# Softmax on one core: whole-tile blocks with one broadcast multiply, one row in eight on ScalarE, and two loads dealt out unevenly

## The chip, the cores and the metric

The kernel runs on one core of a Trainium2 chip. The metric is the time of one execution on the device in microseconds (us), the median of several runs. The work is done by two compute engines, VectorE (DVE in the profile) and ScalarE (ACT), and by 16 DMA engines that move data between the main memory (HBM) and the on-chip memory (SBUF, 128 partitions). Transfers are issued by SyncE (SP, all loads) and by ScalarE (all stores). TensorE and GpSimd do nothing here.

## The reference

`x` has 16 x 1024 rows of 512 float32 values. Each row is divided by a temperature of 0.5 and put through softmax.

```python
def setup_inputs():
    batch, seq, dim = 16, 1024, 512
    return {
        "x": np.random.randn(batch, seq, dim).astype(np.float32),
    }

def reference(x: np.ndarray) -> np.ndarray:
    temp = 0.5
    x_scaled = x / temp
    x_max = np.max(x_scaled, axis=-1, keepdims=True)
    exp_x = np.exp(x_scaled - x_max)
    return (exp_x / np.sum(exp_x, axis=-1, keepdims=True)).astype(np.float32)
```

33.55 MB are read and 33.55 MB written.

## The kernel before

The 16,384 rows are cut into eight tiles (`c` = 0 to 7) of 4 MB. In a tile each of the 128 partitions holds `G` = 16 consecutive rows of 512 values, 32 KB that are contiguous in HBM too. All work is done in place in the tile `xt`; the pool `data` has six such buffers, so tiles 0 to 5 can be loaded at once, and the load of tile 6 has to wait until tile 0 has been stored, that of tile 7 until tile 1 has been.

A tile is worked on in blocks: tile 0 in blocks of 4, 4 and 8 rows, the others in two blocks of 8 rows. For a block there are five steps.

- `shift` (VectorE): one reduce gives the negated maximum of every row (L65), and a small multiply by 2 turns it into a bias (L67).
- `exponentials` (ScalarE): one ACTIVATE a row computes exp(2x + bias) in place and adds the row up into `sums` (L75).
- `scale_vector` (VectorE): a reciprocal of the sums (L89), then one TENSOR_SCALAR a row that multiplies by it (L91), for three rows in four.
- `scale_scalar` (ScalarE): the rest, one row in four, by an ACTIVATE with Copy and a scale (L98).
- `store` (issued on ScalarE's queue, L105): when the tile's last block is done, one 4 MB transfer.

The order is written out by hand: each engine works through its instructions in the order in which the program gives them. The loop runs over the blocks, and each later step lags behind:

```python
for i in range(n + 3):
    if i < n:
        if blocks[i][1] == 0:
            load(blocks[i][0])
        shift(i)
        exponentials(i)
    if 1 <= i <= n:
        scale_vector(i - 1)
    if 2 <= i <= n + 1:
        scale_scalar(i - 2)
    if 3 <= i:
        store(i - 3)
```

So on VectorE the order is shift of block i, scale of block i-1; on ScalarE it is exponentials of block i, Copies of block i-2, store of block i-3. The loads stand alone on SP's queue (L59): tile 0 in three transfers of 1, 3 and 12 rows a partition, the other tiles in one. Transfers signal their end over eight semaphores that loads and stores take in turn; the framework adds the waits.

Of the kernel before, what the change touches and what calls it, by code (L numbers as in the profile page):

```python
# [1 line left out]

# [4 lines left out]


@with_exitstack
def kernel(  # L10
    ctx: ExitStack,
    tc: tile.TileContext,
    x: bass.AP,
    out: bass.AP,
):
    nc = tc.nc
    fp32 = mybir.dt.float32
    P = nc.NUM_PARTITIONS
    AX = mybir.AxisListType.X
    EXP = mybir.ActivationFunctionType.Exp  # L20
    COPY = mybir.ActivationFunctionType.Copy
    MAX = mybir.AluOpType.max

    D = x.shape[-1]
    xf = x.flatten_outer_dims()
    of = out.flatten_outer_dims()
    N = xf.shape[0]

    G = 16
    C = N // (P * G)
    assert C * P * G == N
    xr = xf.rearrange("(c p g) d -> c p g d", p=P, g=G)
    outr = of.rearrange("(c p g) d -> c p g d", p=P, g=G)

    FIRST = [(0, 1), (1, 4), (4, 16)]
    BLOCKS_FIRST = [(0, 4), (4, 4), (8, 8)]
    BLOCKS = [(0, 8), (8, 8)]  # L40

    data = ctx.enter_context(tc.tile_pool(name="data", bufs=6))
    stats = ctx.enter_context(tc.tile_pool(name="stats", bufs=6))

    ctx.enter_context(tc.manual_schedule())


    warm = stats.tile([P, 1], fp32, name="warm", bufs=1)
    nc.vector.memset(warm, 0.0)  # L49
    nc.scalar.activation(out=warm, in_=warm, func=EXP)  # L50

    tiles = {}
    blocks = [(c, b, B) for c in range(C) for b, B in (BLOCKS if c else BLOCKS_FIRST)]
    state = {}

    def load(c):
        xt = tiles[c] = data.tile([P, G, D], fp32, name="xt")
        for lo, hi in FIRST if c == 0 else [(0, G)]:
            nc.sync.dma_start(out=xt[:, lo:hi, :], in_=xr[c][:, lo:hi, :])  # L59

    def shift(i):
        c, b, B = blocks[i]
        xb = tiles[c][:, b : b + B, :]
        negmax = stats.tile([P, 8], fp32, name="negmax")
        nc.vector.tensor_reduce(negmax[:, 0:B], xb, axis=AX, op=MAX, negate=True)  # L65
        bias = stats.tile([P, 8], fp32, name="bias")
        nc.vector.tensor_scalar_mul(bias[:, 0:B], negmax[:, 0:B], 2.0)  # L67
        state[i] = (xb, bias)

    def exponentials(i):  # L70
        B = blocks[i][2]
        xb, bias = state[i]
        sums = stats.tile([P, 8], fp32, name="sums")
        for g in range(B):
            nc.scalar.activation(  # L75
                out=xb[:, g, :],
                in_=xb[:, g, :],
                func=EXP,
                bias=bias[:, g : g + 1],
                scale=2.0,  # L80
                accum_out=sums[:, g : g + 1],
            )
        state[i] = (xb, sums)

    def scale_vector(i):
        B = blocks[i][2]
        xb, sums = state[i]
        recip = stats.tile([P, 8], fp32, name="recip")
        nc.vector.reciprocal(recip[:, 0:B], sums[:, 0:B])  # L89
        for g in range(B - B // 4):  # L90
            nc.vector.tensor_scalar_mul(xb[:, g, :], xb[:, g, :], recip[:, g : g + 1])  # L91
        state[i] = (xb, recip)

    def scale_scalar(i):
        B = blocks[i][2]
        xb, recip = state[i]
        for g in range(B - B // 4, B):
            nc.scalar.activation(  # L98
                out=xb[:, g, :], in_=xb[:, g, :], func=COPY, scale=recip[:, g : g + 1]
            )  # L100

    def store(i):
        c, b, B = blocks[i]
        if b + B == G:
            nc.scalar.dma_start(out=outr[c], in_=tiles[c])  # L105

    n = len(blocks)
    for i in range(n + 3):
        if i < n:
            if blocks[i][1] == 0:  # L110
                load(blocks[i][0])
            shift(i)
            exponentials(i)
        if 1 <= i <= n:
            scale_vector(i - 1)
        if 2 <= i <= n + 1:
            scale_scalar(i - 2)
        if 3 <= i:
            store(i - 3)


# [1 line left out]
_INS = ['x']  # L123
_OUTS = [((16, 1024, 512), 'float32')]


# [23 lines left out]
```

## Time and profile before

| | |
|---|---|
| median of 9 runs | 162.86 us (162.54 to 163.09) |
| the profiled execution's own time | 163.02 us |
| span of the profiled execution | 161.2 us |
| VectorE busy | 114.0 us (71%), 148 instructions |
| ScalarE busy | 113.1 us (70%), 290 instructions |
| data moved by the DMA engines | 67.13 MB, mean 417 GB/s |
| time in packets, share of 16 engines' span | loads 49.4%, stores 48.2% |
| transfers | 10 loads issued on SP, 8 stores issued on ScalarE |

The span is the stretch that the profile covers, from the first to the last instruction; the time has some 1.8 us more around it. A busy share is an average over the whole span. A queue's share is the time that its packets took, over the time of all 16 DMA engines: 100% for loads and stores together would be engines that are never without a packet. In the lines below, "x16" is a number of instructions, "128x512" partitions by elements, and "<-" names what ended a wait.

### The profile page before, as it was taken

What the parts mean: (1) busy time and instruction counts of PE and PEld (TensorE: products, weight loads), DVE (VectorE), ACT (ScalarE), POOL (GpSimd) and SP (SyncE); (2) the same over time, 40 slices, a digit from 0 to 9 for tenths busy, and PEclk for the clock granted to TensorE, in tenths of its full rate; (3) what the DMA queues carried; (4) which work ended last, traced back from release to release, by engine and by line L of the source; (5) the groups of instructions that cost most, each with busy time, mean ns of one, the idle gap of its engine ahead of it and who ended that gap; (6) DMA issues with size and microseconds to landing.
All of it is one profiled execution on the core that took longest, in us unless ns stands there. A gap on an engine that the chain in (4) does not pass through costs nothing.

```text
span 161.2 us, 519 instructions
## 1 busy us (share of the span) xinstructions
DVE 114.0 (71%) x148; ACT 113.1 (70%) x290; POOL 0.2 (0%) x4
## 2 busy tenths in 40 slices
DVE  0507999999999999999999938997099956000000
ACT  3071579989999999999999994699808999200000
POOL 0000000000000000000000000000000000000000
DMA  5999999999999999999999999999999999999993
GB/s 175 476 407 488 407 399 496 409 398 488 407 301 464 392 447 455 399 439 455 407 425 472 407 415 480 407 415 480 407 415 472 415 415 455 431 415 455 431 415 130
DMA packets 2595, 67.13 MB, mean 417 GB/s; under 512 B 288, under 2 KB 288, under 8 KB 544
## 3 DMA queue, kind: packets, MB, share of 16 engines
q1 hardware_dynamic: 1440, 33.56, 49.4%
q10 hardware_dynamic: 1152, 33.55, 48.2%
q14 instruction: 3, 0.02, 0.0%
HBM read 33.55 MB, written 33.55 MB: 416 GB/s over the span
## 4 chain that ended last, share of the span: by engine, by line
DMA 43%; DVE 34%; ACT 7%; issue 1%; SPq 1%
DMA xt<-in_x_dram 25%; DVE negmax L65 23%; DMA out_dram<-xt 19%; DVE xt L91 9%; ACT xt L75 5%; ACT xt L98 2%; DVE bias L67 1%; SPq L59 1%; DVE recip L89 0%
## 5 line engine op out<-in xcount | busy, mean ns | idle before, releaser
L75 ACT ACTIVATE xt<-xt,bias 128x512 f32<-128x512 f32 x128 | 90.5, 708 | 24.2 <-DVE bias L67 24.2
L65 DVE TENSOR_REDUCE negmax<-xt 128x8 f32<-128x4096 f32 (+1 forms) x17 | 70.8, 4165 | 17.9 <-DMA xt<-in_x_dram 17.9
L91 DVE TENSOR_SCALAR xt<-xt,recip 128x512 f32<-128x512 f32 x96 | 39.6, 482 | 0.6
L75 ACT ACTIVATION_READ_ACCUMULATOR xt<-xt,bias 128x1 f32 x128 | 23.9, 187 | 0.0
L98 ACT ACTIVATE xt<-xt,recip 128x512 f32<-128x512 f32 x32 | 21.0, 707 | 0.0
L89 DVE RECIPROCAL recip<-sums 128x8 f32<-128x8 f32 (+1 forms) x17 | 3.3, 193 | 3.2 <-ACT xt L75 3.2
L67 DVE TENSOR_SCALAR bias<-negmax 128x8 f32<-128x8 f32 (+1 forms) x17 | 2.9, 172 | 0.6
L50 ACT ACT_TABLE_LOAD x1 | 1.3, 1283 | 0.7 <-PEq L134 0.7
L49 DVE MEMSET warm<- 128x1 f32 x1 | 0.1, 59 | 0.8 <-PEq L134 0.8
L50 ACT ACTIVATE warm<-warm 128x1 f32<-128x1 f32 x1 | 0.2, 203 | 0.0
L134 POOL MEMSET const-bfloat16-1.0<- 128x1 bf16 x1 | 0.1, 101 | 0.0
L134 POOL MEMSET const-uint8-127<- 128x1 uint8 x1 | 0.1, 101 | 0.0
L134 POOL MEMSET const-float32-0.0<- 128x1 f32 x1 | 0.1, 98 | 0.2 <-issue 0.2
L134 POOL MEMSET const-float32-1.0<- 128x1 f32 x1 | 0.1, 98 | 0.0
## 6 DMA issues: line engine op xcount, KB each, us to landing
out_dram<-xt ACTq DMA_DIRECT2D x8, 4096.0 KB, 26.1
xt<-in_x_dram SPq DMA_DIRECT2D x7, 4096.0 KB, 30.4
xt<-in_x_dram SPq DMA_DIRECT2D x1, 3072.0 KB, 11.2
xt<-in_x_dram SPq DMA_DIRECT2D x1, 768.0 KB, 4.4
xt<-in_x_dram SPq DMA_DIRECT2D x1, 256.0 KB, 2.9
```

The lines of the kernel that those rows point to most:

```text
L49: nc.vector.memset(warm, 0.0)
L50: nc.scalar.activation(out=warm, in_=warm, func=EXP)
L59: nc.sync.dma_start(out=xt[:, lo:hi, :], in_=xr[c][:, lo:hi, :])
L65: nc.vector.tensor_reduce(negmax[:, 0:B], xb, axis=AX, op=MAX, negate=True)
L67: nc.vector.tensor_scalar_mul(bias[:, 0:B], negmax[:, 0:B], 2.0)
L75: nc.scalar.activation(out=xb[:, g, :], in_=xb[:, g, :], func=EXP, bias=bias[:, g : g + 1], scale=2.0, accum_out=sums[:, g : g + 1],)
L89: nc.vector.reciprocal(recip[:, 0:B], sums[:, 0:B])
L91: nc.vector.tensor_scalar_mul(xb[:, g, :], xb[:, g, :], recip[:, g : g + 1])
L98: nc.scalar.activation(out=xb[:, g, :], in_=xb[:, g, :], func=COPY, scale=recip[:, g : g + 1])
L134: nc = _bacc.Bacc("TRN2", target_bir_lowering=False, num_devices=1)
```

## The change

The blocks are redefined: tile 0 keeps blocks of 4, 4 and 8 rows, tiles 1 to 6 are one block of 16 rows each, tile 7 has two of 8. On VectorE the row-by-row multiply becomes one two-tensor multiply a block (L121 after the change), whose second operand is the reciprocal, broadcast along the row. VectorE scales seven rows in eight of a block of eight or more and all rows of a block of four; ScalarE scales the rest (L130).

The order changes too: the shift runs two blocks ahead, the exponentials one block ahead, and block i's multiply, Copies and store are given in the same turn, with the shift of block i+2 between the multiply and the store.

The loads change in tiles 0, 1 and 2. Tile 0 comes in two transfers (4 and 12 rows a partition). Tiles 1 and 2 each come in one transfer of the first 12 rows on all partitions (L76) and five of the last four rows (L81), on 2, 6, 10, 14 and 96 partitions in tile 1 and on 4, 8, 8, 12 and 96 in tile 2. Buffers for tiles 6 and 7 are those of tiles 0 and 1, as before.

```diff
--- before.py
+++ after.py
@@ -34,12 +34,14 @@
     assert C * P * G == N
     xr = xf.rearrange("(c p g) d -> c p g d", p=P, g=G)
     outr = of.rearrange("(c p g) d -> c p g d", p=P, g=G)
+    WHOLE = [(0, G)]
+    LOADS = [[(0, 4), (4, G)]] + [WHOLE] * 7
+    BLOCKS = [[(0, 4), (4, 8), (8, G)]] + [WHOLE] * 6 + [[(0, 8), (8, G)]]
+    STORES = [WHOLE] * 8
+    BMAX = 16
+    BUFS = 6
 
-    FIRST = [(0, 1), (1, 4), (4, 16)]
-    BLOCKS_FIRST = [(0, 4), (4, 4), (8, 8)]
-    BLOCKS = [(0, 8), (8, 8)]
-
-    data = ctx.enter_context(tc.tile_pool(name="data", bufs=6))
+    data = ctx.enter_context(tc.tile_pool(name="data", bufs=BUFS))
     stats = ctx.enter_context(tc.tile_pool(name="stats", bufs=6))
 
     ctx.enter_context(tc.manual_schedule())
@@ -49,74 +51,105 @@
     nc.vector.memset(warm, 0.0)
     nc.scalar.activation(out=warm, in_=warm, func=EXP)
 
-    tiles = {}
-    blocks = [(c, b, B) for c in range(C) for b, B in (BLOCKS if c else BLOCKS_FIRST)]
-    state = {}
+    chunks = {}
+    blocks = [(c, lo, hi) for c in range(C) for lo, hi in BLOCKS[c]]
+    n = len(blocks)
+    biases, sums, recips = {}, {}, {}
 
     def load(c):
-        xt = tiles[c] = data.tile([P, G, D], fp32, name="xt")
-        for lo, hi in FIRST if c == 0 else [(0, G)]:
+        if c < BUFS:
+            chunks[c] = data.tile([P, G, D], fp32, name="xt")
+        else:
+            chunks[c] = chunks[c - BUFS]
+        xt = chunks[c]
+        if c in SPLITS:
+            load_split(c)
+            return
+        for lo, hi in LOADS[c]:
             nc.sync.dma_start(out=xt[:, lo:hi, :], in_=xr[c][:, lo:hi, :])
 
+
+    SPLITS = {1: [2, 6, 10, 14, 96], 2: [4, 8, 8, 12, 96]}
+    LAST = slice(G - 4, G)
+
+    def load_split(c):
+        nc.sync.dma_start(
+            out=chunks[c][:, 0 : G - 4, :], in_=xr[c][:, 0 : G - 4, :]
+        )
+        p = 0
+        for k in SPLITS[c]:
+            nc.sync.dma_start(
+                out=chunks[c][p : p + k, LAST, :], in_=xr[c][p : p + k, LAST, :]
+            )
+            p += k
+        assert p == P
+
     def shift(i):
-        c, b, B = blocks[i]
-        xb = tiles[c][:, b : b + B, :]
-        negmax = stats.tile([P, 8], fp32, name="negmax")
-        nc.vector.tensor_reduce(negmax[:, 0:B], xb, axis=AX, op=MAX, negate=True)
-        bias = stats.tile([P, 8], fp32, name="bias")
-        nc.vector.tensor_scalar_mul(bias[:, 0:B], negmax[:, 0:B], 2.0)
-        state[i] = (xb, bias)
+        c, lo, hi = blocks[i]
+        if c not in chunks:
+            load(c)
+        b = hi - lo
+        negmax = stats.tile([P, BMAX], fp32, name="negmax")
+        nc.vector.tensor_reduce(
+            negmax[:, 0:b], chunks[c][:, lo:hi, :], axis=AX, op=MAX, negate=True
+        )
+        biases[i] = stats.tile([P, BMAX], fp32, name="bias")
+        nc.vector.tensor_scalar_mul(biases[i][:, 0:b], negmax[:, 0:b], 2.0)
 
     def exponentials(i):
-        B = blocks[i][2]
-        xb, bias = state[i]
-        sums = stats.tile([P, 8], fp32, name="sums")
-        for g in range(B):
+        c, lo, hi = blocks[i]
+        sums[i] = stats.tile([P, BMAX], fp32, name="sums")
+        for g in range(hi - lo):
+            row = chunks[c][:, lo + g, :]
             nc.scalar.activation(
-                out=xb[:, g, :],
-                in_=xb[:, g, :],
+                out=row,
+                in_=row,
                 func=EXP,
-                bias=bias[:, g : g + 1],
+                bias=biases[i][:, g : g + 1],
                 scale=2.0,
-                accum_out=sums[:, g : g + 1],
+                accum_out=sums[i][:, g : g + 1],
             )
-        state[i] = (xb, sums)
+
 
     def scale_vector(i):
-        B = blocks[i][2]
-        xb, sums = state[i]
-        recip = stats.tile([P, 8], fp32, name="recip")
-        nc.vector.reciprocal(recip[:, 0:B], sums[:, 0:B])
-        for g in range(B - B // 4):
-            nc.vector.tensor_scalar_mul(xb[:, g, :], xb[:, g, :], recip[:, g : g + 1])
-        state[i] = (xb, recip)
+        c, lo, hi = blocks[i]
+        b = hi - lo
+        k = b - b // 8
+        recips[i] = stats.tile([P, BMAX], fp32, name="recip")
+        nc.vector.reciprocal(recips[i][:, 0:b], sums[i][:, 0:b])
+        rows = chunks[c][:, lo : lo + k, :]
+        nc.vector.tensor_mul(
+            rows, rows, recips[i][:, 0:k].unsqueeze(2).broadcast_to((P, k, D))
+        )
 
     def scale_scalar(i):
-        B = blocks[i][2]
-        xb, recip = state[i]
-        for g in range(B - B // 4, B):
+        c, lo, hi = blocks[i]
+        b = hi - lo
+        for g in range(b - b // 8, b):
+            row = chunks[c][:, lo + g, :]
             nc.scalar.activation(
-                out=xb[:, g, :], in_=xb[:, g, :], func=COPY, scale=recip[:, g : g + 1]
+                out=row, in_=row, func=COPY, scale=recips[i][:, g : g + 1]
             )
 
     def store(i):
-        c, b, B = blocks[i]
-        if b + B == G:
-            nc.scalar.dma_start(out=outr[c], in_=tiles[c])
+        c, _, end = blocks[i]
+        for lo, hi in STORES[c]:
+            if hi == end:
+                nc.scalar.dma_start(
+                    out=outr[c][:, lo:hi, :], in_=chunks[c][:, lo:hi, :]
+                )
 
-    n = len(blocks)
-    for i in range(n + 3):
-        if i < n:
-            if blocks[i][1] == 0:
-                load(blocks[i][0])
-            shift(i)
-            exponentials(i)
-        if 1 <= i <= n:
-            scale_vector(i - 1)
-        if 2 <= i <= n + 1:
-            scale_scalar(i - 2)
-        if 3 <= i:
-            store(i - 3)
+    shift(0)
+    shift(1)
+    exponentials(0)
+    for i in range(n):
+        if i + 1 < n:
+            exponentials(i + 1)
+        scale_vector(i)
+        scale_scalar(i)
+        if i + 2 < n:
+            shift(i + 2)
+        store(i)
 
 
 # ---- launch: one core; inputs and outputs as the reference has them ----
```

## The prediction

> **What bounds the kernel now.** I read the page's slices of the span first, then the windows by stage, then the timeline of the end, then the groups by shape for prices.
>
> The slices: each digit is a fortieth of the span, 4.03 us.
>
> ```profile
> DVE  0507999999999999999999938997099956000000
> ACT  3071579989999999999999994699808999200000
> DMA  5999999999999999999999999999999999999993
> ```
>
> VectorE and ScalarE are full in the middle, but idle in the last seventh. The transfers alone run from end to end. The windows split this by stage (busy us of each engine, clock, DMA share, GB/s):
>
> ```profile
> core 0: us, DVE busy (x) ACT busy (x) POOL busy (x), PEclk, DMA share, GB/s
> 0.00:4.00 4.00, 0.06 (x1) 1.49 (x2) 0.20 (x4) 1.00 0.56 173
> 12.00:44.00 32.00, 30.78 (x39) 24.97 (x67) 0.00 (x0) 1.00 1.02 441
> 44.00:50.00 6.00, 5.93 (x8) 5.84 (x15) 0.00 (x0) 1.00 0.97 339
> 50.00:90.00 40.00, 39.65 (x50) 39.17 (x104) 0.00 (x0) 1.00 1.00 433
> 130.00:158.00 28.00, 3.85 (x10) 8.03 (x20) 0.00 (x0) 1.00 1.00 431
> ```
>
> From 12 us on the DMA share is 1.00, with one dip in bytes where the first store joins the loads (44 to 50). From 130 to 158 us the engines do almost nothing and the rate stays at 431 GB/s. The end of the timeline shows how far ahead they are:
>
> ```profile
> 134.63 2.47 DVE L91 TENSOR_SCALAR xt<-xt,recip 128x512 f32<-128x512 f32 x6
> 135.61 0.34 ACTq L105 DMA_DIRECT2D out_dram<-xt  x1
> 136.10 1.93 ACT L98 ACTIVATE xt<-xt,recip 128x512 f32<-128x512 f32 x3
> 138.06 0.34 ACTq L105 DMA_DIRECT2D out_dram<-xt  x1
> ```
>
> The last store is issued at 138.06 and lands at 160.3. Its packets need 8 x 1.21 = 9.7 us on each DMA engine, so it stands 12 us behind earlier stores. **The bound is the 67.13 MB on the DMA engines.** The chain of waits names VectorE for a third of the span, but with a queue that never empties those steps set nothing. So three things can move the time: transfer time lost at the start, what the fullest DMA engine carries, and a queue that runs dry.
>
> The packet records say more on the second. A 32 KB packet takes 1.213 us, 24 KB 0.912, 8 KB 0.309, 4-byte semaphore packets 0.009. Laid end to end they make 16 chains, one per DMA engine, each with 128 rows' worth of 32 KB. Thirteen chains end between 158.32 and 158.95 us (mean 158.66), the others at 159.40, 159.42 and 159.90. The last sets the span of 161.2. It holds two of three 8 KB packets of queue 14 (at 31.7 and 83.1 us), the 159.40 one the third (54.5 us); the 159.42 one has none, and I don't know why it is late.
>
> [...]
>
> **The change part by part.** Prices from the groups by shape:
>
> ```profile
> L75 ACT ACTIVATE xt<-xt,bias 128x512 f32<-128x512 f32 x128 | 90.5, 708 | 24.2 <-DVE bias L67 24.2
> L65 DVE TENSOR_REDUCE negmax<-xt 128x8 f32<-128x4096 f32 x15 | 66.2, 4415 | 8.4 <-DMA xt<-in_x_dram 8.4
> L91 DVE TENSOR_SCALAR xt<-xt,recip 128x512 f32<-128x512 f32 x96 | 39.6, 482 | 0.6
> L98 ACT ACTIVATE xt<-xt,recip 128x512 f32<-128x512 f32 x32 | 21.0, 707 | 0.0
> ```
>
> *VectorE.* 96 one-row multiplies (0.412 us apart in the chain: 39.6 us) go. In come 11 multiplies over 113 rows, [...] the rate at which the reduce reads (4.34 us for 4096 elements): 60.3 us plus about 0.1 each. Reduces lose six starts. From tile 0's second landing, now about 12.4, VectorE works nearly without a gap: 124 rows of reduce 66.1, ten reduces' overhead with the small multiply 0.28 each 2.8, the scales 60.3 and 11 x 0.19 = 2.1, and 1.9 us of waiting for the last exponentials: it ends near 145.6, against 137.1 before.[...] *ScalarE* loses 16 Copies, 11.3 us; it isn't the bound: nothing. The store now stands right behind the Copies on ScalarE and waits for the multiply, with the next exponentials queued behind it. These wait for a shift that follows the same multiply on VectorE: nothing.
>
> *The cover.* Stores are issued near 44.5, 58, 74, 91, 107, 124, 131 and 145.6. With loads and stores sharing the engines in turn, each store finds the one before it still moving; the seventh ends at about 148.4. A transfer's first packet comes 1.0 us after its issue (0.73 to 1.72 for the first load), so the last store joins at 146.6: 1.8 to 2 us of cover[...]. If it is gone, each us late costs one.
>
> *SP* issues 19 transfers for 10, at about 0.43 us. From the ninth on each waits for a semaphore whose earlier load has landed; at each such wait at least a 12-row load of 7.3 us is still queued, so the cost is nothing; a gap would cost 1 to 1.4 us. Tiles 6 and 7 still wait for stores 0 and 1.
>
> *Start.* The first 1 MB comes in one transfer instead of two. Before, tile 0's packets ended at 11.94 to 12.49, mean 12.26, though packets that follow each other at once would need 9.8 us from a start at 1.72 to 2.28, so 11.8. **Gain 0.5 us** (bounds 0.2 and 0.6).
>
> *The split loads.* In tiles 1 and 2 one packet per partition becomes two: 0.912 + 0.310 for 1.213, times 16, plus up to ten semaphore packets: **loss 0.2 us** on each chain. [...] **Engines 0 and 1 carry 4 x 0.310 = 1.24 us more**, engines 14 and 15 as much less.[...]
>
> *Refills.* VectorE goes from 148 instructions to 46 and loses its refill, on a chain that isn't the last; ScalarE keeps two (290 to 273).
>
> *Sum.* Fullest engine: 158.66 - 0.5 + 0.2 + 1.24 = 159.6, against 159.9: -0.3 us, if ScalarE's refills fall on an engine with a number above 7 (then that chain ends at or below 159.6). The profiled execution takes 163.02 (span 161.2 and 1.8 around it), 0.16 above the median; on the median 162.86 - 0.3 = 162.56, say **162.5**[...].
>
> **The rivals.** About 0.2%, 0.33 us, is what a measurement can tell from no change here.
> - *A, as summed* (0.50): its own range 161.9 to 163.0. For it: the chains' ends lie within 0.6 us but for three. Against: that spread is as large as the gain.
> - *E, the late chains are the high-numbered ones* and the skew evens them: -0.8 us or more, 162.0 (0.08). No record names an engine's number.
> - *B, ScalarE's refills fall on a low-numbered engine*: 159.9 - 0.3 + 0.62 to 1.24 gives +0.3 to +0.9, 163.5 (0.15).
> - [...]
> - *D, VectorE becomes the bound.* The place is the last multiply of tile 7; it decides from 2 us over 113 rows, 18 ns a row, so at 551 ns for 533. At 570 ns: 4.2 - 2 = +2.2 and no gain, 165.0 (0.10). For it: no broadcast operand was measured.[...]
> - The change not doing what it says: if narrow loads spread over all 16 engines there is no skew, and E's time comes out.
>
> **How the numbers follow.** Faster: 0.33 of A and all of E, 0.41. Same: 0.14 of A, 0.03 of B, 0.02 of C, 0.19. Slower: 0.03 of A, 0.12 of B, 0.15 of C and D's 0.10, 0.40. The range takes A, E, B and the lower half of C and D: 161.8 to 164.2.
>
> **What would show it.** Right: DMA share 1.00 from 12 us to the end, last store issued by 147.5, a multiply of 14 rows in 7.5 to 7.7 us, first shift near 5.2 instead of 5.65, packets of tiles 1 and 2 at 0.31 us, and chain ends fanned over some 2.4 us. Wrong: 8 KB packets of 0.6 us and more (C), a DMA digit below 9 ahead of the last store (D), or chains that end together (E).

## The result, and the profile after

The changed kernel takes **169.45 us** (median of 9 runs, 169.11 to 170.70) against 162.76 us for the kernel before in the same measurement: a ratio of 1.0417, 95% interval 1.0402 to 1.0431. A ratio leaves out runs more than 1.5% above the fastest of their kernel, which is one run in all, of experiment 8. The forecast was 162.5 us with a range to 164.2; its rival C (0.17) was that the narrow loads slow each other down. The profiled execution took 169.57 us, with a span of 167.8.

The slices of the page of the kernel after; one slice is now 4.2 us.

```profile
DVE  0509988997999999999999999499984999959000
DMA  5999999999999999999999999999999999995893
GB/s 197 428 469 445 316 268 416 305 273 377 445 430 430 430 430 438 438 430 445 414 430 438 430 439 438 422 453 406 445 414 453 414 445 430 430 438 250 383 492 133
```

Two things are new. In slices 5 to 9 (17 to 38 us) the bytes fall to 268 and 273 GB/s while the DMA digit stays at 9: the DMA engines hold packets all the time, and the packets take longer (0.563 us for 0.309, below). And in slice 37 (151 to 155 us) the DMA digit is 5: the queue runs dry just ahead of the end. The windows by stage of the same kernel (busy us of each engine, clock, DMA share, GB/s) separate the two:

```profile
core 0: us, DVE busy (x) ACT busy (x) POOL busy (x), PEclk, DMA share, GB/s
20.00:26.00 6.00, 4.70 (x5) 3.73 (x11) 0.00 (x0) 1.00 1.05 279
26.00:31.00 5.00, 5.00 (x1) 2.01 (x6) 0.00 (x0) 1.00 1.00 428
31.00:38.00 7.00, 6.93 (x4) 3.20 (x9) 0.00 (x0) 1.00 1.06 253
38.00:150.00 112.00, 104.59 (x29) 83.73 (x227) 0.00 (x0) 1.00 1.00 431
150.00:157.00 7.00, 4.09 (x2) 2.08 (x6) 0.00 (x0) 1.00 0.68 295
157.00:167.80 10.80, 0.00 (x0) 0.00 (x0) 0.00 (x0) 1.00 0.79 340
```

20 to 26 and 31 to 38 us are the stretches in which the narrow loads of tiles 1 and 2 move. At 430 GB/s their bytes would have needed (1 - 279/430) x 6 + (1 - 253/430) x 7 = 2.1 + 2.9 = 5.0 us less. Between them (26 to 31) the wide part of tile 2 runs at 428. The packet records say the same from below: of the 256 narrow packets of 8 KB the mean is 0.563 us, where such a packet takes 0.309 with all partitions in the transfer.

The end of the timeline, after:

```profile
145.21 3.89 DVE L121 TENSOR_TENSOR xt<-xt,recip 128x3584 f32<-128x3584 f32 x1
...
150.89 0.20 DVE L119 RECIPROCAL recip<-sums 128x8 f32<-128x8 f32 x1 [1.78 <-ACT xt L104]
151.12 3.89 DVE L121 TENSOR_TENSOR xt<-xt,recip 128x3584 f32<-128x3584 f32 x1
155.10 0.34 ACTq L138 DMA_DIRECT2D out_dram<-xt  x1
```

The last store is issued at 155.10 and lands at 166.8. It is late because tile 7's load landed only at 128.1: from there VectorE still has 27.0 us to do (128.1 to 155.1), the shifts and multiplies of the last tiles and a wait of 1.78 us. The chain of waits holds that load as one piece:

```profile
89.60 38.48 DMA xt<-in_x_dram
```

Tile 7's load has 16 completions, one for each DMA engine: ten by 123.2 us, five more by 125.5, and the last, of the engine that also carried ScalarE's instruction refills, at 128.1. VectorE's next reduce starts at 128.10: it waits for the fullest engine.

The refills are the 8 KB packets of queue 14, which the page calls `instruction`: two here, three before. I take the two for ScalarE's, which starts 125 instructions between them and VectorE 15 (in the kernel before, 131 of ScalarE between the two on the latest chain), and the third for VectorE's, whose instructions fell from 148 to 45.

Laid end to end as chains, one for each DMA engine, the chain of packets with both of ScalarE's instruction refills (at 40.1 and 100.1 us) has no gap and ends last, at 166.47. The other 15 stand idle for 0.7 to 3.4 us ahead of about 156.0, then carry the last store to 165.7 to 165.8. So two things hold the end, 0.7 us apart: the fullest DMA engine, and the late last store.

The durations of the operations were close to those priced; the groups by shape of the kernel after:

```profile
L104 ACT ACTIVATE xt<-xt,bias 128x512 f32<-128x512 f32 x128 | 90.4, 707 | 49.2 <-DVE bias L97 49.2
L93 DVE TENSOR_REDUCE negmax<-xt 128x16 f32<-128x8192 f32 x6 | 52.1, 8682 | 4.4 <-DMA xt<-in_x_dram 4.4
L121 DVE TENSOR_TENSOR xt<-xt,recip 128x7168 f32<-128x7168 f32 x6 | 45.7, 7625 | 0.2
L130 ACT ACTIVATE xt<-xt,recip 128x512 f32<-128x512 f32 x15 | 9.9, 706 | 0.0
```

A multiply of 14 rows takes 7.625 us, 545 ns a row with its fixed part. ScalarE now waits 49.2 us for biases (24.2 before), which costs nothing while the DMA engines are full: they hold packets in every slice from 4.2 to 151 us (digit 9).

### The profile page after: what moved, and what is told of

The parts are those of the page before. It is cut to its first block, busy times and chain, and to the rows that moved or that the text cites. A ratio compares the mean times of both kernels' runs of the same rounds, so it can differ in the third digit from the quotient of the medians.

```text
span 167.8 us, 422 instructions
## 1 busy us (share of the span) xinstructions
DVE 135.0 (80%) x45; ACT 102.1 (61%) x273; POOL 0.2 (0%) x4
## 3 DMA queue, kind: packets, MB, share of 16 engines
q1 hardware_dynamic: 1648, 33.56, 50.5%
## 4 chain that ended last, share of the span: by engine, by line
DMA 62%; DVE 18%; ACT 10%; SPq 1%; issue 1%; DVEq 0%; ACTq 0%
DMA xt<-in_x_dram 45%; DMA out_dram<-xt 17%; DVE negmax L93 10%; ACT xt L104 10%; DVE xt L121 7%; ACT xt L130 1%; SPq L69 0%; SPq L81 0%; DVE bias L97 0%; SPq L76 0%; DVE recip L119 0%; DVEq L93 0%; ACTq L104 0%
## 5 line engine op out<-in xcount | busy, mean ns | idle before, releaser
L104 ACT ACTIVATE xt<-xt,bias 128x512 f32<-128x512 f32 x128 | 90.4, 707 | 49.2 <-DVE bias L97 49.2
L93 DVE TENSOR_REDUCE negmax<-xt 128x16 f32<-128x8192 f32 (+2 forms) x11 | 69.9, 6355 | 16.7 <-DMA xt<-in_x_dram 16.7
L121 DVE TENSOR_TENSOR xt<-xt,recip 128x7168 f32<-128x7168 f32 (+2 forms) x11 | 62.0, 5637 | 0.4
L130 ACT ACTIVATE xt<-xt,recip 128x512 f32<-128x512 f32 x15 | 9.9, 706 | 0.0
L119 DVE RECIPROCAL recip<-sums 128x16 f32<-128x16 f32 (+2 forms) x11 | 2.4, 219 | 1.8 <-ACT xt L104 1.8
L97 DVE TENSOR_SCALAR bias<-negmax 128x16 f32<-128x16 f32 (+2 forms) x11 | 1.9, 173 | 0.4
```

The source lines that it names most:

```text
L93: nc.vector.tensor_reduce(negmax[:, 0:b], chunks[c][:, lo:hi, :], axis=AX, op=MAX, negate=True)
L97: nc.vector.tensor_scalar_mul(biases[i][:, 0:b], negmax[:, 0:b], 2.0)
L104: nc.scalar.activation(out=row, in_=row, func=EXP, bias=biases[i][:, g : g + 1], scale=2.0, accum_out=sums[i][:, g : g + 1],)
L119: nc.vector.reciprocal(recips[i][:, 0:b], sums[i][:, 0:b])
L121: nc.vector.tensor_mul(rows, rows, recips[i][:, 0:k].unsqueeze(2).broadcast_to((P, k, D)))
L130: nc.scalar.activation(out=row, in_=row, func=COPY, scale=recips[i][:, g : g + 1])
```

## The experiments

Each edit is against the kernel after unless another is named. The kernel before ran on the same chip each time, at a median of 162.67 to 162.72 us.

**1. The change without its split loads.** Theory P, here and in experiments 2 to 4, is that the loads on few partitions slow each other down, and that the rest of the loss follows from it.

```diff
-    SPLITS = {1: [2, 6, 10, 14, 96], 2: [4, 8, 8, 12, 96]}
+    SPLITS = {}
```

> The changed kernel with tiles 1 and 2 loaded whole, in one transfer each; all else as changed. Theory P[...]: no packet of 8 KB above 0.35 us after tile 0, the last store issued near 145.6, DMA share 1.00 to the end, 162.4 to 162.8 us. Rival V (the two-tensor multiply and the new order make the last store late, splits or not): last store at 150 or later, a gap in the DMA share before it, 165 us or more. Rival S (pieces of the last four rows are slow as such) expects what P does here.

Measured: 162.37 us, ratio 0.9982 (0.9975 to 0.9990). Page and end of the timeline of this kernel:

```profile
DMA  5999999999999999999999999999999999999993
```

```profile
143.44 3.89 DVE L121 TENSOR_TENSOR xt<-xt,recip 128x3584 f32<-128x3584 f32 x1
147.41 0.34 ACTq L138 DMA_DIRECT2D out_dram<-xt  x1
```

No digit below 9 until the last slice, and the store goes out at 147.41. The whole loss of 7 us is gone with the split loads; VectorE's new work and order don't cause it. This version also has the lowest median of all that were measured and beats both kernels, if by little: 0.18% under the kernel before, with an interval that excludes 1. Its chains end at 158.0 to 158.3, the one with the refills at 159.16.

**2. The split loads alone, in the kernel before.**

```diff
--- before
+    SPLITS = {1: [2, 6, 10, 14, 96], 2: [4, 8, 8, 12, 96]}
...
+        if c in SPLITS:
+            nc.sync.dma_start(out=xt[:, 0 : G - 4, :], in_=xr[c][:, 0 : G - 4, :])
+            p = 0
+            for k in SPLITS[c]:
+                nc.sync.dma_start(
+                    out=xt[p : p + k, G - 4 : G, :], in_=xr[c][p : p + k, G - 4 : G, :]
+                )
+                p += k
...
+            return
```

> The kernel before with nothing changed but the loads of tiles 1 and 2, which are cut as in the changed kernel. P: the same 8 KB packets of 0.55 to 0.6 us, some 4 to 5 us lost on each DMA engine, 1.2 more on the fullest; before has 12 us of stores queued ahead of its last one, so no gap at the end: 167 to 168.5 us. V: the splits cost only their own packets, 163 to 164 us. S: as P.

Measured: 172.75 us, ratio 1.0623 (1.0608 to 1.0637), several us above what any theory said. The slices of the page and two windows of this kernel:

```profile
DMA  5999999999999999999999999999999489498985
```

```profile
20.00:26.00 6.00, 5.93 (x7) 4.43 (x13) 0.00 (x0) 1.00 1.05 261
...
120.00:140.00 20.00, 14.90 (x19) 14.61 (x39) 0.00 (x0) 1.00 0.83 359
```

The slow narrow packets are there again (261 GB/s). What was missed is the end: before's order keeps the stores of tiles 5, 6 and 7 all behind tile 7's load, the first of them behind the exponentials of that tile's first block. They go out at 137.07, 148.97 and 151.42, and the DMA engines run dry ahead of the first and again ahead of the second (the digits of 4). In the kernel before, tile 6's store goes out 18.8 us after that load has landed (116.8 to 135.61); here too (130.1 to 148.97), and from then two stores of 4 MB need 20.9 us to their landing at 169.8. With the load at 116.8 this sum ends at 156.5 and hides behind the queue; with the load at 130.1 it is the end.

**3. Packets just as small and at the same place, but on all partitions.**

```diff
+    SPLITS = {1: [128], 2: [128]}
```

> The changed kernel with tiles 1 and 2 each in two transfers over all 128 partitions, the first 12 rows and the last four: the same 8 KB pieces at the same places, dealt evenly. P: packets of 0.31 us, 162.5 to 163.0 us, as without splits but for 0.15 us of extra packets. S: packets of 0.57 us, 4 us lost, 166 us or more. V: 165 us or more.

Measured: 162.57 us, ratio 0.9991 (0.9983 to 0.9999). The window of experiment 1, and the same one of this kernel:

```profile
19.00:26.00 7.00, 6.93 (x5) 3.79 (x11) 0.00 (x0) 1.00 1.04 449
```

```profile
19.00:26.00 7.00, 6.93 (x5) 3.74 (x11) 0.00 (x0) 1.00 1.01 431
```

All 256 packets of 8 KB take 0.309 to 0.321 us. So neither their size, nor the place of these rows in HBM, nor the cut of a load in two is the cause; the packets took longer (0.563 us) where the same rows were loaded by transfers over only some of the partitions.

**4. Narrow, but dealt out evenly.** The last four rows go in transfers of 32 and 96 partitions. That this deals them out evenly shows in the result: all 16 chains end 3.7 to 4.1 us later than in experiment 1.

```diff
+    SPLITS = {1: [32, 96], 2: [32, 96]}
```

> The changed kernel with the last four rows of tiles 1 and 2 in two transfers, on 32 and on 96 partitions.[...] P: the packets are as slow as with the five transfers (0.55 to 0.6 us)[...], but no engine is fuller than another: 4 us lost on all, 1.2 less on the fullest, 165.5 to 168 us. If it is the narrow transfers (2 to 14 partitions) alone that collide: 0.31 us, 162.6 us. S: 0.57 us. V: 165 us or more.

Measured: 166.11 us, ratio 1.0207 (1.0187 to 1.0226). The slices of the page and two windows of this kernel:

```profile
DMA  5999999999999999999999999999999999999992
```

```profile
19.00:26.00 7.00, 6.42 (x5) 3.63 (x11) 0.00 (x0) 1.00 1.05 311
...
31.00:38.00 7.00, 6.93 (x4) 3.81 (x11) 0.00 (x0) 1.00 1.02 300
```

Packets take 0.533 and 0.542 us in the mean: (0.533 + 0.542 - 2 x 0.309) x 8 = 3.7 us for each DMA engine (8 of a tile's 128 packets), and the time is 3.7 us above experiment 1. There is no gap ahead of the last store (issued at 149.6). So with nothing uneven the longer packets alone cost 3.7 us. The other 3.3 us come with the five transfers of the changed kernel, which are dealt out unevenly; four of the five are also narrower than 32 partitions, and no run sets these two apart.

**5. The first load alone, in the kernel before.**

```diff
--- before
-    FIRST = [(0, 1), (1, 4), (4, 16)]
+    FIRST = [(0, 4), (4, 16)]
```

> The kernel before with tile 0 loaded in two transfers (4 and 12 rows) instead of three, nothing else. If the prediction's start term holds, every DMA engine ends 0.5 us earlier: 162.2 us. Against it: without the splits the changed kernel's tile 0 landed at 12.3 to 12.7 us against 12.3 to 12.9 before, which gives 0.1 to 0.2 us: 162.5 to 162.7 us.

Measured: 162.66 us against 162.72, ratio 0.9995 (0.9984 to 1.0005). The half a us that the prediction gave to the start isn't there.

**6. Which partitions: sixteen neighbours, or every eighth.** One run. Tile 1 tries sixteen neighbours a transfer, tile 2 every eighth partition, tile 3 two halves of 64. I expected the neighbours to be much the slowest.

```diff
+    SPLITS = {
+        1: [slice(16 * j, 16 * j + 16) for j in range(8)],
+        2: [slice(j, P, 8) for j in range(8)],
+        3: [slice(0, 64), slice(64, P)],
+    }
...
```

> The changed kernel with the last four rows dealt evenly in other ways: tile 1 in eight transfers of 16 neighbouring partitions (0 to 15, 16 to 31, ...), tile 2 in eight of every eighth partition (0, 8, 16, ...), tile 3 in two of 64 partitions.[...] Read are the packets' durations.[...] If any transfer over fewer than 128 partitions is slow for another reason: 0.57 us in all three tiles.

Measured: 170.98 us. The medians of the 8 KB packets are 0.638, 0.595 and 0.605 us in tiles 1, 2 and 3. In tile 1 the first packets took up to 1.08 us, but the median lies within 8% of the other two. So the neighbours are not the much slower ones that I had expected, and the packets are slow in all three tiles (0.309 over all partitions, experiment 3).

**7. Which DMA engines the refills use.** One run. Tiles 1 and 2 are loaded whole; tile 4's load is cut into transfers of 112, 2, 2, 2, 2 and 8 partitions, so that the two engines that a transfer over two partitions uses carry more than the others (such a load had two completions after the one at its issue in the changed kernel). The text on record takes these two for engines 0 and 1, so rival B would have a refill on one of them; no record names an engine's number.

```diff
+    SPLITS = {4: [112, 2, 2, 2, 2, 8]}
...
-                out=chunks[c][p : p + k, LAST, :], in_=xr[c][p : p + k, LAST, :]
+                out=chunks[c][p : p + k, :, :], in_=xr[c][p : p + k, :, :]
```

> The changed kernel with tiles 1 and 2 loaded whole and tile 4 dealt out unevenly: whole rows of 32 KB on 112, 2, 2, 2, 2 and 8 partitions. [...] so two chains of packets fall behind all others by 4 us and more. Rival B (ScalarE's instruction refills fall on a low-numbered engine): one of these two chains holds the refill packet near 98 us. If the refills are on another engine: neither of the two does.

Measured: 181.69 us. Two of 16 chains fall behind: tile 7's load landed on 14 engines by 130.8 us and on the other two at 139.1 and 140.6. The later of the two is 0.76 us behind the other when tile 5's load lands (101.21 and 100.45) and 1.45 when tile 6's does (121.25 and 119.80) and from there on; ScalarE's second refill, at 109.2, lies between. So that refill is on one of these two engines.

**8. The splits in the kernel before, with each store ahead of the next turn.** Against experiment 2.

```diff
--- experiment 2
+        if 3 <= i:
+            store(i - 3)
         if i < n:
...
-        if 3 <= i:
-            store(i - 3)
```

> The kernel before with the split loads (172.75 us), and each store given at the start of the next turn instead of its end, ahead of the exponentials of the next block. With the split loads the store of tile 5 was issued at 137.07, behind exponentials of tile 7 that waited for its late load, and the DMA engines ran dry before it. Theory: the order costs what the splits' kernel lost over the changed kernel; without that wait no gap before the store of tile 5, 169 to 170.5 us. If the order doesn't matter: 172.5 us or more.

Measured: 175.25 us (173.16 to 178.02), ratio 1.0694 (1.0644 to 1.0743): no faster, and slower if anything (experiment 2 took 172.62 to 173.14). **The theory fell.** It took the position of the stores in the turn for the cause of experiment 2's excess. A window of this kernel:

```profile
142.00:152.00 10.00, 6.69 (x13) 9.60 (x24) 0.00 (x0) 1.00 0.22 95
```

The dry stretch only moved to 142 to 152 us. Tile 7's load landed at 133.0 instead of 130.1, and the store of tile 6 again followed it by 18.8 us (151.8). The edit freed only the store of tile 5, which went out at 132.43, ahead of that landing and not 7 us behind it; tile 6's still stands behind the exponentials of tile 7's second block. So this run shows that the place in the turn isn't enough, not that the order plays no part. The first store went out 2.1 us earlier (41.9 for 44.0), so loads had to share the DMA engines earlier. That this delayed tile 7 fits, but was not tried by itself.

**9. All rows on VectorE, in experiment 1.** This tests how much cover VectorE's chain has.

```diff
+    SPLITS = {}
...
-        k = b - b // 8
+        k = b
...
-        for g in range(b - b // 8, b):
+        for g in range(b, b):
```

> The changed kernel with tiles 1 and 2 loaded whole, and VectorE scaling all 16 rows of a tile (no Copies on ScalarE). Without the splits VectorE's last store was issued at 147.41 us while the store before it was moving until 148.4 or so: the cover of the prediction, now nearly used up. 15 more rows at 0.53 us make VectorE's chain 8 us longer. If VectorE is at the edge, as the prediction's rival D has it, every us shows: last store near 155.3, a gap in the DMA share before it, 169.5 to 170.5 us. If there is still cover: under 168 us.

Measured: 168.57 us, ratio 1.0365 (1.0350 to 1.0381). The windows of this kernel near the end:

```profile
140.00:142.00 2.00, 2.00 (x1) 0.00 (x0) 0.00 (x0) 1.00 0.61 262
...
150.00:156.00 6.00, 4.63 (x2) 0.19 (x2) 0.00 (x0) 1.00 0.20 87
```

VectorE works through while the DMA engines stand. The last store went out 7.55 us later than in experiment 1 (154.96 for 147.41), and the chains end at 165.6 to 165.7 for 158.0 to 158.3: but for the one with the refills, they are later by the same 7.5 us, so VectorE had no cover left. Two chains of experiment 1 already stand for 0.09 and 0.12 us ahead of the last store's packets. The time rose by 6.2 only, because experiment 1 ended with the refills' chain, at 159.16 some 1.0 us behind the others.

**10. The order of the sixteens.** One run. The same 16-partition loads as in tile 1 of experiment 6, in two other orders. I expected tile 1 to be slower than the rising order of experiment 6, and tile 2 faster.

```diff
+    SPLITS = {
+        1: [slice(s, s + 16) for s in (0, 32, 16, 48, 64, 96, 80, 112)],
+        2: [slice(s, s + 16) for s in (0, 64, 16, 80, 32, 96, 48, 112)],
+    }
...
```

> The changed kernel with the last four rows of tiles 1 and 2 in eight transfers of 16 neighbouring partitions each, the same transfers in both but in another order[...]. In rising order such packets took 0.64 us, after a first wave of up to 1.08.[...] If any transfer over fewer than 128 partitions is slow for another reason: 0.6 to 0.65 in both.

Measured: 172.14 us. A window of this kernel, and the same one of experiment 6:

```profile
19.00:26.00 7.00, 5.53 (x4) 3.77 (x11) 0.00 (x0) 1.00 1.06 148
```

```profile
19.00:26.00 7.00, 5.70 (x4) 3.60 (x11) 0.00 (x0) 1.00 1.01 227
```

Tile 1's packets rise from a median of 0.638 us in the rising order to 0.971 by their order alone, as expected. Tile 2's took 0.745, slower than the rising order and not faster: half of what I expected holds. If a transfer's width alone set the time, both would have stayed near 0.64.

**11. Extra packets on the same two engines, in experiment 1.** Four extra loads of two partitions go into a buffer that nothing reads: four more packets, counted at 4 x 0.31 = 1.24 us, on each of the two engines that experiment 7 loaded.

```diff
+    spare = data.tile([P, 4, D], fp32, name="spare", bufs=1)
...
+        if c == 1:
+            for p in (0, 2, 4, 6):
+                nc.sync.dma_start(
+                    out=spare[p : p + 2, :, :], in_=xr[0][p : p + 2, 0:4, :]
+                )
...
+    SPLITS = {}
```

> The changed kernel with tiles 1 and 2 loaded whole and four small loads added behind tile 1's, of two partitions and 8 KB each, into a buffer that nothing reads[...]. Without them the chain with ScalarE's refills ended at 159.2, all others at 158.0 to 158.3. If the refills are on engine 0 or 1 (rival B): that chain ends at 160.4 or later, 163.4 to 164.2 us. If on another engine: engines 0 and 1 end at 159.3, level with it, 162.4 to 162.7 us.

Measured: 164.68 us, ratio 1.0133 (1.0112 to 1.0154), 2.3 us above experiment 1. Two chains end at 161.29 and 161.32, the other 14 at 158.3 to 158.7. No third chain is late, so the refills lie in the two that were loaded. The size was missed: the four packets cost 1.5 and 1.6 us in a chain where 1.24 was counted, and the chains end 2.9 us behind the rest. These eight packets, though on two partitions each transfer, had a median of 0.324 us: among wide loads on the other engines narrow packets were mostly not slow, so narrowness as such is not enough; what made the others slow is not shown. Why the two end together, though in experiment 1 the refills made one chain late and not two, stays open.

**12. Where to, or where from.** One run. In tile 1 the partitions written are in the order of experiment 10's tile 1 (`PAIRED`) and the rows read in rising order, in tile 2 the reverse. 0.97 us in tile 1 and 0.6 in tile 2 would speak for the order of writing.

```diff
+    RISING = (0, 16, 32, 48, 64, 80, 96, 112)
+    PAIRED = (0, 32, 16, 48, 64, 96, 80, 112)
+    SPLITS = {1: list(zip(PAIRED, RISING)), 2: list(zip(RISING, PAIRED))}
...
+                out=chunks[c][to : to + 16, LAST, :],
+                in_=xr[c][of : of + 16, LAST, :],
```

> As the run with sixteens in another order, with the two sides of a transfer set apart: in tile 1 the partitions written go in pairs[...] (0, 32, 16, 48, 64, 96, 80, 112) while the places read in HBM go in rising order, in tile 2 the other way round. The last four rows of these two tiles so come from other partitions' rows, which changes what the output holds there and no amount of work. In rising order on both sides a packet took 0.64 us (median), paired on both sides 0.97.[...] If it is the order in which HBM is read: 0.6 in tile 1, 0.97 in tile 2.

Measured: 173.28 us. Tile 1's packets have a median of 0.975 us, tile 2's 0.773. The order of the partitions written is what makes 0.97, at both orders of reading that were tried; with the partitions rising, the order of reading gives 0.773 in tile 2 here, against 0.638 in tile 1 of experiment 6. What makes this second, smaller part isn't settled.

## Why the prediction was wrong, and where it was right

**The step that failed first** is "one packet per partition becomes two: 0.912 + 0.310 for 1.213". The narrow packets were priced like wide ones, with no measurement behind it: no load of before was narrow. A narrow packet took 0.563 us for 0.309, 16 of them on an average DMA engine: 4.06 us. Rival C, that they slow each other down, had a price that was my estimate and rested on no run, and the range took in its lower half alone, to 164.2; in fact every engine paid (in experiment 4, dealt out evenly, all 16 chains end 3.7 to 4.1 us later than in experiment 1). Experiment 3 shows that it takes transfers over part of the partitions (0.309 to 0.321 us over all 128), experiment 4 that this alone costs 3.7 us (0.533 and 0.542 us a packet), experiments 10 and 12 that the order of the partitions written matters (0.971 and 0.975 us, 0.638 in rising order). Experiment 11 adds that narrow packets among wide loads were mostly not slow (0.324 us). What happens inside isn't shown.

**The skew** was priced at "4 x 0.310 = 1.24 us". The four were my assumption. The completions of the kernel after agree: 2, 6, 10, 14 and 16 for the loads of 2, 6, 10, 14 and 96 partitions of tile 1, besides one at the issue of each but the last, and 4, 8, 8, 12 and 16 in tile 2. An engine in all five loads of a tile would carry 1 + 1 + 1 + 1 + 6 = 10 narrow packets where 8 are even. The price was that of a wide packet: at 0.563 the four are 2.25. The fullest engines then have 20 narrow packets, by the mean packet 20 x 0.563 - 16 x 0.309 = 6.3 us more than 16 wide ones (an estimate, since no record names a packet's engine).

**The condition of the sum**, "if ScalarE's refills fall on an engine with a number above 7", was false: they fall on one of the two engines that a transfer over two partitions uses (experiments 7 and 11), and these, by the estimate above, have the 20 packets. The two add up. From experiment 1's refill chain, 159.16 + 6.3 = 165.5; that chain ended at 166.47. The last 1.0 us I put to longer packets around the narrow ones, which wasn't tried by itself: between 23 and 39 us packets of 24 KB took up to 1.7 us for 0.912, and of 32 KB up to 2.2 for 1.213. From experiment 4, whose refill chain ends at 163.27, it is 3.2 us: 2.25 would be the four packets, and what makes the rest was not set apart.

**VectorE's cover** was worked out as 1.8 to 2 us and was nothing against the 15 chains without both refills (experiment 9). The predicted store at 145.6 came at 147.41 without the splits; 1.7 us of this are the multiplies, 62.0 us together where 60.3 was counted. Those 60.3 are 113 rows at 533 ns, which the reduces of the kernel before show: 4.415 us for 4096 elements (the prediction's line) and 2.286 for 2048 are 532 ns a row apart.

```profile
L65 DVE TENSOR_REDUCE negmax<-xt 128x4 f32<-128x2048 f32 x2 | 4.6, 2286 | 9.5 <-DMA xt<-in_x_dram 9.5
```

The multiplies kept that rate: 7.625 us for 14 rows and 3.892 for 7 are 533 ns a row apart. The fixed part, "about 0.1 each" and left out of the sum, was some 0.16 each, 1.7 us in all.

With the splits the cover was not the point: the landing of tile 7's load was. It has to be there by about 147.4 - 27.0 = 120.4 us if the last store is not to move, and came at 128.1 (114.7 in experiment 1). That lateness was larger than the time lost. In the median of the 16 engines, tile 3's landing was 6.3 us behind experiment 1 (47.9 for 41.6), tile 7's 10.5 (122.9 for 112.4), and its last engine, with the uneven deal and the refills, came another 5.2 us after that. From about 50.5 us on, load packets and store packets share the engines (210 GB/s of loads and 222 of stores from 60 to 90 us, where loads alone moved at 413 from 38 to 50.5), which fits a load that gets through its backlog at half the rate. The prediction named the shift of this kind as a rival only for a slow multiply ("VectorE becomes the bound"), not as a follower of the narrow loads.

**The start**, "Gain 0.5 us", was 0.06, not to be told from nothing (experiment 5). Tile 0's packets ended at 12.14 us in the mean for 12.26. What was read as a gap is for the most part first packets that take longer, and those stay: with one issue less the 8 KB packets of tile 0 took 0.359 us in the mean for 0.309 (0.373 in the changed kernel).

**Right** were: that before is bound by its bytes on the DMA engines; the count of four extra narrow packets on the fullest engines, as far as the completions show it; the multiply, predicted at 7.5 to 7.7 us; the refill taken for VectorE's gone (two instruction packets for three); that ScalarE's fewer Copies and its waits cost nothing, nor SP's extra issues: no slice ahead of 150 us is dry. Without the narrow loads the rest gives 162.37 for 162.67, the -0.3 us of the sum, but this agreement is luck: the sum had a start gain of 0.5 in it that isn't there, and a skew against it that isn't in this version either.

Of the rivals, C had the right sign to watch, 8 KB packets of 0.6 us and more, and B held as well. Each was costed as if it came alone.

## What to carry to other kernels

Deal a load over all 128 partitions: cutting it into pieces of 96 partitions and fewer made their packets longer here, from 0.31 to 0.53 us or more in the mean, even when no DMA engine carried more than another (experiment 4). In a kernel bound by its transfers, look for the fullest chain of packets, and count what lands on the same engine together (refills, uneven shares) as a sum and not as alternatives. When loads and stores take turns, a load that is late at the start can be later still at its landing (6.3 us became 10.5 here), so ask of each load by when the last store needs it, and count its landing on the fullest engine.

## What was not expected of the hardware

- The same sixteen-partition loads took 0.638 or 0.971 us a packet by their order alone (experiments 6 and 10).
- ScalarE's refills, 8 KB of 0.309 us each and only two of them, hold the end of a kernel that moves 67 MB: 159.16 us against 158.0 to 158.3 for the other chains in experiment 1. The 32 KB packets right behind them took 1.575 and 1.461 us there for 1.213, so a refill cost its engine about twice its own packet.
- With the first store issued 2.1 us earlier, the load of tile 7 landed 2.9 us later and the kernel was no faster (experiment 8, 175.25 us against 172.75).
